# The GLA state-times-query product on operands split in two, in two of three token blocks

## The chip, the cores and the metric

One core of a Trainium2 chip runs the whole program. The metric is the device time of one execution in microseconds (us); the kernel before has a median of 1791.93 us over three runs (1784.84 to 1792.70).

## The reference, cut to what matters

One decoder layer over 2048 prompt tokens and 64 sample tokens, width 1024. A projection `x @ w_in` feeds two branches, a sliding-window attention and a gated linear attention (GLA); both are gated, projected, merged and normalised. The GLA branch is what the change touches. It has 4 heads with 128 key channels and 256 value channels, and walks over chunks of tokens with a state `S` (128 x 256) per head:

```
def step(S, xs):
    qc, kc, vc, gc = xs
    b = jnp.cumsum(gc, axis=1)
    b_last = b[:, -1]
    qt = qc * jnp.exp(b)
    kt = kc * jnp.exp(-b)
    kend = kc * jnp.exp(b_last[:, None] - b)
    o_inter = jnp.einsum('bthk,bhkv->bthv', qt, S)
    A = jnp.where(causal, jnp.einsum('bthk,bshk->bhts', qt, kt), 0.0)
    o_intra = jnp.einsum('bhts,bshv->bthv', A, vc)
    S = jnp.exp(b_last)[..., None] * S + jnp.einsum('bshk,bshv->bhkv', kend, vc)
    return S, o_inter + o_intra
```

The kernel takes chunks of 128 tokens. `o_inter`, the state times the query, is the product that changes.

## The kernel before, in words

**The matrix products.** All tokens (2112) are cut in three token blocks `s` = 0, 1, 2 of 704. The main loop runs over `groups`: each is one weight block times one activation block, 4 (or 2) k-steps of three matmuls each (L1326, L1327, L1328), since every operand is held as a high and a low part in the 32-bit type fp32r and the product is high*high + high*low + low*high. `split` (L142, L143) makes the parts: ScalarE casts the value to fp32r, and VectorE subtracts that from the value. Most products use a seven-product scheme, whose sums of weight blocks GpSimd makes (L348) and whose sums of activation blocks VectorE makes (`cx`, L465). The loop order is the order on TensorE, and it is fixed by hand. On the other engines and on SyncE's DMA queue a list scheduler sets the order at build time.

**The side work.** Attention and GLA ride along: `at(t, f)` files a function under a tick, one tick is four k-steps of the main loop (12 matmuls), and `tick()` runs what is due. GLA work for block `s` is filed by `gla_phase`: for each head and each piece of up to 256 tokens a dictionary `B`, and for each of its chunks `i`, `st` ticks apart, `gla_v` and `gla_a`, then 5/3 `st` later `gla_b`, then 10/3 `st` after the first `gla_c`. Before these come the loads of the piece (`gla_load`, `gla_load_v`: `gin`, `zkq`, `zvv`), `gla_z` (a scan and exponentials of the gates, L1030 to L1047) and, three ticks ahead of the first chunk, `gla_kq`, which multiplies keys and queries with them (L1058, L1060). Its result `qb` lies in the tile named `gb`.

**The product.** `gla_b` opens a PSUM accumulation with `qb` times the state in plain fp32 (L1110), adds the three products of the split scores `ah` and values `gv`, `gl` (L1104, through `three`), makes the state update in a second PSUM tile in the same way, and VectorE then writes the new state (L1118). The outputs of the first chunk of a head in block 0 have no state product.

**Tiles.** `mtile("fin")` is the ring of result tiles: ten tiles of 128 x 352 in which the results of the main loop wait for their way to memory (`fin`, `th`, `part`), and which the gate work also uses (`zg`, `gin`). `wp` are six tiles of split weights, `ws` ten of raw ones, `r` the raw activations from `xT`. The main loop writes four PSUM tiles `pd` in turn, the side work four named `pa`.

Of the kernel before, what the change touches and what calls it, by code (L numbers as in the profile page):

```python
# [13 lines left out]
F32R = mybir.dt.float32r  # L14
# [24 lines left out]
HV = 256  # L39
# [4 lines left out]
MS = NT // (2 * MT)  # L44
# [13 lines left out]
def kernel(ctx, tc, io):  # L58
    nc = tc.nc
    mm = nc.tensor.matmul  # L60
# [15 lines left out]
    def pa():  # L76
        return psa.tile([P, 512], F32, tag="pa", name="pa")

    T = MT

    def mtile(tag, dt=F32, name=None):
        n, bufs = {"xb": (4 * T, 16), "a": (T, 7), "fin": (T, 10), "ws": (512, 10), "wp": (D, 6)}[tag]
        pool = px if tag == "xb" else pr
        return pool.tile([P, n], dt, tag=tag, name=name or tag, bufs=bufs)
# [6 lines left out]
    def mpool(name):  # L91
        mid.close()
        M["name"] = name
        M["p"] = mid.enter_context(tc.tile_pool(name=name, bufs=1, side="left", reuse_waits="tile"))

    def mt(tag, n, bufs, dt=F32, name=None):
        return M["p"].tile([P, n], dt, tag=tag, name=name or tag, bufs=bufs)
# [26 lines left out]
    def at(t, fn):  # L124
        side.setdefault(max(int(t), now[0]), []).append(fn)
# [15 lines left out]
    def split(dst_h, dst_l, src, eng=nc.vector):  # L141
        pin["a"] = nc.scalar.copy(dst_h, src)  # L142
        i = eng.tensor_tensor(dst_l, src, dst_h.bitcast(F32), ALU.subtract)  # L143
        if eng is nc.vector:
            pin["d"] = i
# [111 lines left out]
    for n, (kind, s, kh, prs) in enumerate(sets):  # L257
        start_of.append(len(groups))
        base.append(int(tk))
        for pr_ in prs:  # L260
# [5 lines left out]
            elif seq[n] in PLAIN:  # L266
                jk = [(j, k) for j in range(2) for k in range(2)]
                for c in range(2):
                    for j, k in jk if kind == "a" else [(j, k) for k, j in jk]:
                        q, p = pr_[j]  # L270
# [428 lines left out]

    def gate_load(B):  # L700
        x = B["x"] = mtile("fin", name="gin")
        s, t = B["s"], B["t"]
        g = gl_d.rearrange("(a b r) t -> b a r t", a=2, b=2)[t][:, :16, s * T:(s + 1) * T]
        for h in range(GH):
            nc.sync.dma_start(x[32 * h:32 * h + 32], g)

    def gate(B, h0):
        ps = [pa() for _ in range(2)]
        for j in range(2):
            r = slice(32 * (h0 + j), 32 * (h0 + j) + 32)  # L710
            mm(ps[j][:, :T], wgk[r], B["x"][r], start=True, stop=True, tile_position=(32 * (h0 + j), 0))
        for j in range(2):
            h = h0 + j
            z, m = B["z", h], B["m", h] = mtile("fin", name="zg"), mt("lg", T, 4, name="mg")
            nc.scalar.activation(z, ps[j][:, :T], AF.Abs, bias=bgk[:, h:h + 1])
            nc.scalar.activation(m, ps[j][:, :T], AF.Relu, scale=-1.0, bias=nbgk[:, h:h + 1])
# [263 lines left out]
    S_t = [const.tile([P, HV], F32, name=f"S{i}") for i in range(GH + 1)]  # L980
# [11 lines left out]
    def rot(key):  # L992
        r = R[key][cnt[key] % len(R[key])]
        cnt[key] += 1
        return r

    sstate = {}
# [56 lines left out]
    def gla_kq(B):  # L1054
        T, Tp = B["T"], B["Tp"]
        zk, zq = B["zkq"][:, 0], B["zkq"][:, 1]
        for t in (B["k"], B["k2"]):
            nc.vector.tensor_tensor(t[:, :T], zk[:, :T], t[:, :T], ALU.mult)  # L1058
        for t, n in ((B["q"], T), (B["qb"], Tp)):
            nc.vector.scalar_tensor_tensor(t[:, :n], zq[:, :n], HK ** -0.5, t[:, :n], ALU.mult, ALU.mult)  # L1060

    def gla_v(B, i):
        n = P if i < B["nt"] else NS
        ts = slice(i * P, i * P + n)
        tp = pa()
        for m in range(2):
            nc.tensor.transpose(tp[:n, m * P:(m + 1) * P], B["zvv"][:, m, ts], ident)  # L1067
        nc.tensor.transpose(tp[:n, HV:HV + HK], B["k2"][:, ts], ident)
        if n == P:
            B["gv", i] = rot("gv"), rot("gl")  # L1070
            split(*B["gv", i], tp[:, :HV + HK])
            return
        g = mt("pr2", 2 * GU, 6, name="gs")[:, :HV + HK]
        nc.scalar.copy(g[:n], tp[:n, :HV + HK])
        nc.vector.tensor_copy(g[NS:], tp[:n, :HV + HK])
        B["gv", i] = g[:, :HV], g[:, HV:]

    def gla_a(B, i):
        ts = slice(i * P, (i + 1) * P)
        ap = pa()  # L1080
        mm(ap[:, :P], B["k"][:, ts], B["q"][:, ts], start=True, stop=True)  # L1081
        A_ = rot("a")
        nc.vector.copy_predicated(A_, cmask.bitcast(U32), ap[:, :P])
        x = rot("ah")
        split(x[:, :P], x[:, P:], A_, nc.gpsimd)
        B["a", i] = x[:, :P], x[:, P:]

    def gla_norm(B, key, o, n):
# [6 lines left out]
        nc.scalar.mul(on[:n], o, sq[:n])  # L1095
        B["on", key] = on

    def gla_b(B, i):
        ts = slice(i * P, (i + 1) * P)
        gh, gl = B["gv", i]  # L1100

        def three(ps, w, x, start):
            for j, (a, c) in enumerate(((w[0], x[0]), (w[1], x[0]), (w[0], x[1]))):
                mm(ps, a, c, start=start and j == 0, stop=(j == 2))  # L1104

        gv, kT2 = (gh[:, :HV], gl[:, :HV]), (gh[:, HV:], gl[:, HV:])
        S = sstate.get(B["h"])
        op = pa()
        if S is not None:
            mm(op[:, :HV], B["qb"][:, ts], S_t[S], start=True, stop=False)  # L1110
        sp = pa()
        three(sp[:, :HV], kT2, gv, True)
        three(op[:, :HV], B["a", i], gv, S is None)
        Sn = S_free.popleft()
        if S is None:
            nc.vector.tensor_copy(S_t[Sn], sp[:, :HV])
        else:
            nc.vector.scalar_tensor_tensor(S_t[Sn], S_t[S], B["e1"][:, i:i + 1], sp[:, :HV], ALU.mult, ALU.add)  # L1118
            S_free.append(S)
        sstate[B["h"]] = Sn  # L1120
        gla_norm(B, i, op[:, :HV], P)
# [59 lines left out]
    def gla_phase(s, t0, st):  # L1181
        at(t0, lambda: mpool(f"cg{s}"))
        at(t0, rings)
        nu = sum(-(-T_ // P) for _, T_ in GCH[s]) * GH
        b0 = t0 + 14
        u = 0
        for h, (c0, T_) in ([(h, c) for c in GCH[s] for h in range(GH)] if s == 1 else
                            [(h, c) for h in range(GH) for c in GCH[s]]):
            if True:
                last = c0 + T_ == NT  # L1190
                Tp = T_ - (NS if last else 0)
                nt = Tp // P
                B = dict(h=h, t0=c0, T=T_, Tp=Tp, nt=nt, last=last)
                tt = lambda v: b0 + st * v + 0.01
                b = tt(u)
                at(b - 13, lambda B=B: gla_load(B))
                at(b - 10, lambda B=B: gla_load_v(B))
                at(b - 8, lambda B=B: gla_z(B))
                at(b - 3, lambda B=B: gla_kq(B))
                for i in range(nt):  # L1200
                    at(tt(u + i), lambda B=B, i=i: gla_v(B, i))
                    at(tt(u + i), lambda B=B, i=i: gla_a(B, i))
                    at(tt(u + i + 5 / 3), lambda B=B, i=i: gla_b(B, i))
                    at(tt(u + i + 10 / 3), lambda B=B, i=i: gla_c(B, i, P, i * P))
                at(tt(u + 1) + 3, lambda B=B: gla_load_g(B))
                o = tt(u + nt)
                u += nt
                if last:
                    u += 1
                    at(o - 5, lambda B=B: samp_state(B))  # L1210
                    at(o, lambda B=B: gla_v(B, B["nt"]))
                    at(o + 2, lambda B=B: samp_a(B))
                    at(tt(u - 1 + 0.5) + 2, lambda B=B: nc.sync.dma_start(io["o_sp"][B["h"]], S_t[sstate[B["h"]]]))
                    o = max(o + 6, tt(u - 1 + 4 / 3) + 1)
                    at(o, lambda B=B: samp_b(B, 0))
                    at(o + 2, lambda B=B: samp_b(B, 2))
                    at(o + 5, lambda B=B: gla_c(B, "s", NS, B["Tp"]))
                    at(max(o + 6, tt(u + 4 / 3) + 1), lambda B=B: gla_store(B))
                else:
                    at(tt(u + 7 / 3) + 1, lambda B=B: gla_store(B))  # L1220
        return int(b0 + st * (nu + 7 / 3) + 3)

    for s in range(MS):
        for t in range(2):
            B = dict(s=s, t=t)
# [6 lines left out]
    t0 = 90  # L1232
    tiles = [sum(-(-n // P) for _, n in c) * GH for c in GCH]
    st = (base[U2] - 3 - t0 - 160 - 17 * MS) / sum(n + 7 / 3 for n in tiles)
    for s in range(MS):
        t0 = gla_phase(s, att_phase(s, t0), st)
# [55 lines left out]
    def rest_m(t, u, n, last):  # L1292
        return [part(f, samples=last) for f in load_m(t, u, n, last)]
# [5 lines left out]
    for g, (n, q, i, s, p, b, ch) in enumerate(groups):  # L1299
# [15 lines left out]
        w = wps.pop(g)  # L1315
# [3 lines left out]
        ps = (banks[b] if b < 4 else banks2[b - 4])[:, :T]  # L1319
        if n == U2 and g >= start_of[U2] + 16:  # L1320
            ps = banks2[b][:, :T]
        for k in range(q.kh):
            ks, ts = slice(k * P, (k + 1) * P), slice(k * T, (k + 1) * T)
# [12 lines left out]
        if n == U2:  # L1336
# [7 lines left out]
            if d == 3:  # L1344
                ox = M["p"]
                xf, x, xr0 = load_m(1, 0, TM), [], []
# [101 lines left out]
    for j, (t, u, n) in enumerate(order):  # L1448
# [9 lines left out]
        for r in tiles:  # L1458
            if r is tiles[-1] and j + 1 < len(order):
                x = rest_m(*order[j + 1], last=(j + 2 == len(order)))  # L1460
# [124 lines left out]
```

## Time and profile before

| | before |
|---|---|
| median of three runs | 1791.93 us (1784.84 to 1792.70) |
| the profiled execution | 1783.34 us, its span 1781.6 us |
| busy: PE, DVE, ACT, POOL | 1752.0, 1085.9, 851.7, 374.5 us |
| granted TensorE clock, mean | 0.997 |

The profile is of one execution. PE is TensorE's matmuls and PEld its weight loads; DVE is VectorE, ACT ScalarE, POOL GpSimd, SP the queue from which most DMAs are issued. A row of a group gives line, engine, operation, output and input tile, shapes, count, then busy time and mean duration, then idle time before it and what ended that. Since matmuls overlap, the duration of one is more than the time to the start of the next; the cost on PE is read from starts. `x2` at a plain fp32 matmul stands for two records of one instruction. GLA of block 0 lies between about 350 and 590 us, of block 1 between about 765 and 1035 us, of block 2 after 1200 us. Line numbers are those of the kernel before.

### The profile page before, as it was taken

The page shows a single profiled execution, that of the slowest core. Times are in us where ns is not written, and L with a number is a line of the kernel's source. Part 1 is how long each engine was busy: PE and PEld are TensorE (multiplying, and loading weights), DVE is VectorE, ACT ScalarE, POOL GpSimd, SP SyncE. Part 2 cuts the span into 40 slices and gives each one's busy share as a digit, 9 for nine tenths or more (in the row PEclk, how much of TensorE's full clock was granted, in tenths as well). Part 3 has the DMA queues.
Part 4 walks back from the last instruction along what each step waited for, and adds up shares of the span by engine and source line. Part 5 has one row for each costly group of instructions (what it writes and reads, how often), then busy time and mean ns, then how long its engine had stood idle before and what let it go on. Part 6 is the DMA issues. An engine that isn't in the chain of part 4 may idle for free.

```text
span 1781.6 us, 31643 instructions
## 1 busy us (share of the span) xinstructions
PE 1752.0 (98%) x11026; PEld 1644.8 (92%) x11026; DVE 1085.9 (61%) x2146; ACT 851.7 (48%) x2052; POOL 374.5 (21%) x522
## 2 busy tenths in 40 slices
PE   8999999998999999999999999999999999999998
PEld 8999988997999988999999998899999999998887
DVE  6656678778555466547655336635766755536666
ACT  4575656556574365446567334645533432311100
POOL 5345533454111000004211100000123132111111
PEclk9999999999999999999999999999999999999999
DMA  6789966976978987887789798779989978965531
GB/s 216 272 317 332 330 232 224 319 279 207 311 261 279 304 258 231 269 286 228 255 266 319 239 294 279 237 244 318 298 267 244 301 212 223 332 148 194 171 104 54
DMA packets 290911, 452.33 MB, mean 254 GB/s; under 512 B 29213, under 2 KB 210133, under 8 KB 290736
## 3 DMA queue, kind: packets, MB, share of 16 engines
q1 hardware_dynamic: 262896, 415.04, 70.7%
q10 hardware_dynamic: 20464, 26.24, 4.2%
q0 software_dynamic: 7392, 9.04, 3.6%
q8 instruction: 87, 1.43, 0.3%
q14 instruction: 72, 0.59, 0.1%
HBM read 297.52 MB, written 153.57 MB: 253 GB/s over the span
## 4 chain that ended last, share of the span: by engine, by line
PE 74%; DMA 2%; DVE 1%; POOL 1%; ACT 1%; issue 1%; SPq 0%; DVEq 0%; ACTq 0%; POOLq 0%
PE pd L1326 17%; PE pd L1328 17%; PE pd L1327 16%; PE pd L1389 3%; PE pd L1390 3%; PE pd L1391 3%; PE pa L1104 2%; PE pa L1110 1%; PE pa L777 1%; PE pa L823 1%; PE pa L809 1%; PE pa L1127 1%; DMA r<-ug_d 1%; PE pa L1067 1%; PE pa L1081 1%; PE pa L1326 1%
## 5 line engine op out<-in xcount | busy, mean ns | idle before, releaser
L143 DVE TENSOR_TENSOR wp<-ws,wp 128x512 fp32r<-128x512 f32 (+1 forms) x396 | 274.4, 696 | 203.9 <-ACT wp L142 192.9
L142 ACT CAST wp<-ws 128x512 fp32r<-128x512 f32 (+1 forms) x396 | 234.2, 595 | 191.8 <-PE pd L1328 127.7
L348 POOL TENSOR_TENSOR ws<-ws 128x256 f32<-128x256 f32 x162 | 144.1, 918 | 156.5 <-DVE wp L143 103.9
L143 POOL TENSOR_TENSOR ah<-aper,ah 128x128 fp32r<-128x128 f32 x64 | 37.3, 583 | 397.6 <-ACT ah L142 394.4
L384 ACT COPY m<-pd 128x352 f32<-128x352 f32 x146 | 66.1, 454 | 87.2 <-PE pd L1328 80.0
L1390 PE MATMUL pd<-woh,x 128*128 128x512 f32 (+1 forms) x272 | 102.4, 377 | 0.0
L1391 PE MATMUL pd<-wol,x 128*128 128x512 f32 (+1 forms) x272 | 102.4, 377 | 0.0
L1389 PE MATMUL pd<-woh,x 128*128 128x512 f32 (+1 forms) x272 | 102.4, 377 | 0.0
L1326 PE MATMUL pd<-x1h,wp 128*128 128x352 f32 x292 | 96.7, 331 | 2.3 <-DVE fin L405 2.2
L1326 PE MATMUL pd<-x7h,wp 128*128 128x352 f32 x292 | 97.1, 333 | 1.1 <-DVE fin L201 0.9
L1326 PE MATMUL pd<-x3h,wp 128*128 128x352 f32 x292 | 96.8, 331 | 0.3 <-DVE fin L399 0.3
L1326 PE MATMUL pd<-x5h,wp 128*128 128x352 f32 x292 | 96.6, 331 | 0.0
L1326 PE MATMUL pd<-x6h,wp 128*128 128x352 f32 x292 | 96.3, 330 | 0.0
L1326 PE MATMUL pd<-x2h,wp 128*128 128x352 f32 x292 | 96.3, 330 | 0.0
L1326 PE MATMUL pd<-x4h,wp 128*128 128x352 f32 x292 | 96.2, 330 | 0.0
L1328 PE MATMUL pd<-x1h,wp 128*128 128x352 f32 x292 | 94.0, 322 | 0.1
L1328 PE MATMUL pd<-x7h,wp 128*128 128x352 f32 x292 | 94.0, 322 | 0.0
L1328 PE MATMUL pd<-x4h,wp 128*128 128x352 f32 x292 | 93.8, 321 | 0.0
L1328 PE MATMUL pd<-x3h,wp 128*128 128x352 f32 x292 | 93.8, 321 | 0.0
L1327 PE MATMUL pd<-x7l,wp 128*128 128x352 f32 x292 | 93.8, 321 | 0.0
L1328 PE MATMUL pd<-x6h,wp 128*128 128x352 f32 x292 | 93.8, 321 | 0.0
L1328 PE MATMUL pd<-x5h,wp 128*128 128x352 f32 x292 | 93.8, 321 | 0.0
(454 smaller groups left out, 5387.9 us busy)
## 6 DMA issues: line engine op xcount, KB each, us to landing
wp<-wk_w_g SPq DMA_DIRECT2D x96, 512.0 KB
ws<-w_g SPq DMA_DIRECT2D x120, 256.0 KB
wk_w_g<-wp SPq DMA_DIRECT2D x48, 512.0 KB
wp<-wk_w_ra SPq DMA_DIRECT2D x32, 512.0 KB
wp<-wk_w_rg SPq DMA_DIRECT2D x32, 512.0 KB
ws<-w_at SPq DMA_DIRECT2D x53, 256.0 KB
wp<-wk_w_at SPq DMA_DIRECT2D x24, 512.0 KB
ws<-w_pg SPq DMA_DIRECT2D x48, 256.0 KB
```

The source lines that it names most:

```text
L142: pin["a"] = nc.scalar.copy(dst_h, src)
L143: i = eng.tensor_tensor(dst_l, src, dst_h.bitcast(F32), ALU.subtract)
L348: nc.gpsimd.tensor_tensor(o[:, c], x[:, c], y[:, c], op)
L384: nc.scalar.copy(A[i], ps)
L777: mm(ps[kv][:, j, k0:], A["zq"][r, g0 + j, :], A["kk"][r, 0, k0:], start=True, stop=True, tile_position=(kv * HD, 0))
L1104: mm(ps, a, c, start=start and j == 0, stop=(j == 2))
L1326: mm(ps, wh, xh[:, ts], start=first, stop=False, skip_group_check=ch)
L1327: mm(ps, wh, xl[:, ts], start=False, stop=False, skip_group_check=ch)
L1328: mm(ps, wl, xh[:, ts], start=False, stop=(k == q.kh - 1 and not (type(i) is tuple and i[1] == 0)), skip_group_check=ch)
L1389: mm(ps, xh[:, xs], hi, start=(k == 0), stop=False)
L1390: mm(ps, xl[:, xs], hi, start=False, stop=False)
L1391: mm(ps, xh[:, xs], lo, start=False, stop=(k == KT - 1))
```

## The change

In blocks 0 and 1 the state product is made like the others: query and state are split in high and low parts, and three fp32r matmuls take the place of one fp32 matmul. Block 2 keeps the fp32 product.

```
--- before.py
+++ after.py
@@ gla_kq
             nc.vector.scalar_tensor_tensor(t[:, :n], zq[:, :n], HK ** -0.5, t[:, :n], ALU.mult, ALU.mult)
+        if B["s"] < MS - 1:
+            B["qs"] = [mtile("fin", F32R, n) for n in ("qbh", "qbl")]
+            split(B["qs"][0][:, :T], B["qs"][1][:, :T], B["qb"][:, :T])
@@
+    def gla_s(B):
+        S = sstate.get(B["h"])
+        if S is not None and "qs" in B:
+            B["Ss"] = [mt(n, HV, 1, F32R) for n in ("Sh", "Sl")]
+            split(*B["Ss"], S_t[S])
+
     def gla_b(B, i):
...
-        def three(ps, w, x, start):
+        def three(ps, w, x, start, last=True):
             for j, (a, c) in enumerate(((w[0], x[0]), (w[1], x[0]), (w[0], x[1]))):
-                mm(ps, a, c, start=start and j == 0, stop=(j == 2))
+                mm(ps, a, c, start=start and j == 0, stop=(last and j == 2))
...
-        if S is not None:
+        if S is not None and "qs" in B:
+            three(op[:, :HV], [q[:, ts] for q in B["qs"]], B["Ss"], True, False)
+        elif S is not None:
             mm(op[:, :HV], B["qb"][:, ts], S_t[S], start=True, stop=False)
@@ gla_phase
-                B = dict(h=h, t0=c0, T=T_, Tp=Tp, nt=nt, last=last)
+                B = dict(s=s, h=h, t0=c0, T=T_, Tp=Tp, nt=nt, last=last)
...
                     at(tt(u + i), lambda B=B, i=i: gla_a(B, i))
+                    at(tt(u + i + 1), lambda B=B: gla_s(B))
                     at(tt(u + i + 5 / 3), lambda B=B, i=i: gla_b(B, i))
```

The query's parts `qbh` and `qbl` take two tiles of the ring `fin` per piece, from `gla_kq` to the piece's last `gla_b`. The state's parts `Sh` and `Sl` have one buffer each; they are made anew for each chunk, two thirds of `st` ahead of its `gla_b`. Block 0 has 20 chunks of which 16 have a state, block 1 has 24: 40 products change. There are 24 pieces, 20 of 256 tokens and 4 of 128.

On PE the place of one such product, in block 0, before:

```order
L1328 MATMUL pd_74<-x5h,wp 128x352
L1110 MATMUL pa<-S_219,gb 128x256
L1104 MATMUL pa<-gv 128x256
L1104 MATMUL pa<-gv,gl 128x256
L1104 MATMUL pa<-gl,gv 128x256
L1104 MATMUL pa<-gv,ah 128x256 x2
L1104 MATMUL pa<-gl,ah 128x256
```

and now:

```order
L1340 MATMUL pd_74<-x5h,wp 128x352
L1113 MATMUL pa<-Sh,qbh 128x256
L1113 MATMUL pa<-Sh,qbl 128x256
L1113 MATMUL pa<-Sl,qbh 128x256
L1113 MATMUL pa<-gv 128x256
L1113 MATMUL pa<-gv,gl 128x256
L1113 MATMUL pa<-gl,gv 128x256
L1113 MATMUL pa<-gv,ah 128x256 x2
L1113 MATMUL pa<-gl,ah 128x256
```

One row becomes three, and nothing else on PE moves. On the other engines the list scheduler places the 128 new instructions and shifts others. On SP's queue in block 0, before (`zkq`, `zvv` and `gin` are loads of later GLA pieces, `ws` raw weights, `r` raw activations, `wk_w_rg` stores of split weights, `sg` a load of the gate of the output):

```order
L314 DMA ws<-w_at 128x512
L1012 DMA zkq<-z_kq_89 128x2x256
L314 DMA ws<-w_at 128x512
L442 DMA r_4676<-xT 128x4x352
L371 DMA wk_w_rg_4602<-wp 128x1024
L371 DMA wk_w_rg_4641<-wp 128x1024
L1009 DMA gin<-zg_d 128x256
L314 DMA ws<-w_at 128x512 x2
L1018 DMA zvv<-z_vv_93 128x2x256
```

and now:

```order
L314 DMA ws<-w_at 128x512
L1012 DMA zkq<-z_kq_89 128x2x256
L1018 DMA zvv<-z_vv_93 128x2x256
L1009 DMA gin<-zg_d 128x256
L314 DMA ws<-w_at 128x512
L442 DMA r_4698<-xT 128x4x352
L371 DMA wk_w_rg_4620<-wp 128x1024
L371 DMA wk_w_rg_4663<-wp 128x1024
L314 DMA ws<-w_at 128x512 x2
```

The loads `zvv` and `gin` now stand ahead of the load of `r`. On DVE a little later, ahead of the write of the state that ends the stretch, before:

```order
L1047 COPY e_4932<-gb 128x2
L1058 TENSOR_TENSOR em<-zkq,em 128x256
L143 TENSOR_TENSOR wp<-ws,wp 128x512
L1058 TENSOR_TENSOR ek<-zkq,ek 128x256
L1060 SCALAR_TENSOR_TENSOR dm<-zkq,dm 128x256
L143 TENSOR_TENSOR x4l<-cx,x4h 128x704
L1060 SCALAR_TENSOR_TENSOR gb<-zkq,gb 128x256
L143 TENSOR_TENSOR x4l<-cx,x4h 128x704
L1118 SCALAR_TENSOR_TENSOR S_223<-S_222,e_4472,pa 128x256
```

and now:

```order
L1047 COPY e_4970<-gb 128x2
L465 TENSOR_TENSOR cx<-r_4917,cx 128x704
L1140 TENSOR_TENSOR sg<-pa,sg 128x2x128
L143 TENSOR_TENSOR wp<-w_4972,wp 128x512
L143 TENSOR_TENSOR wp<-ws,wp 128x512
L465 TENSOR_TENSOR cx<-r_4917,cx 128x704
L143 TENSOR_TENSOR x4l<-cx,x4h 128x704
L143 TENSOR_TENSOR wp<-ws,wp 128x512
L143 TENSOR_TENSOR x4l<-cx,x4h 128x704
L1129 SCALAR_TENSOR_TENSOR S_223<-S_222,e_4484,pa 128x256
L143 TENSOR_TENSOR wp<-ws,wp 128x512
L1058 TENSOR_TENSOR em<-zkq,em 128x256
```

The seven steps of `gla_z` and `gla_kq` that one piece had in this stretch on DVE (L1030, L1035, L1036, L1058 twice, L1060 twice) now stand before or behind it: the scan, `dm` and both steps on `ek` ahead of the step on `cx` that waits for `r`, the other three behind the write of the state. The split of this chunk's state (`Sl`) stands four rows ahead of the piece shown.

## The prediction

> **What bounds the kernel now.** First the page's busy times, then the stretches in which the change acts.
>
> ```profile
> span 1781.6 us, 31643 instructions
> PE 1752.0 (98%) x11026; PEld 1644.8 (92%) x11026; DVE 1085.9 (61%) x2146; ACT 851.7 (48%) x2052; POOL 374.5 (21%) x522
> ```
>
> TensorE is busy nearly all of the time; DVE and ACT have room on average. An average hides stages, so the second view is the busy time by stretch (columns: stretch, length, then PE, PEld, DVE, ACT, POOL with their counts, granted clock, DMA share, GB/s).
>
> ```profile
> core 0: us, PE busy (x) PEld busy (x) DVE busy (x) ACT busy (x) POOL busy (x), PEclk, DMA share, GB/s
> 340.00:396.00 56.00, 55.04 (x356) 54.15 (x355) 40.60 (x74) 34.28 (x81) 24.48 (x35) 1.00 0.86 303
> 396.00:430.00 34.00, 27.62 (x179) 23.38 (x178) 30.43 (x56) 21.80 (x52) 18.55 (x22) 0.95 0.58 183
> 430.00:600.00 170.00, 170.00 (x1102) 165.98 (x1101) 88.16 (x197) 95.84 (x229) 25.98 (x47) 1.00 0.85 278
> 740.00:1040.00 300.00, 300.00 (x1959) 293.25 (x1959) 169.71 (x354) 167.06 (x398) 51.93 (x88) 1.00 0.82 271
> ```
>
> Two regimes. From 430 to 600 and from 740 to 1040 PE is never idle: time saved on PE comes off the end, and DVE and ACT are 52 to 57% busy. From 396 to 430 PE is idle for 6.4 of 34 us while DVE is 90% busy: there the other engines set the pace. PE's waits over both say who is late:
>
> ```profile
> PE pd L1326 <- DVE fin L405: 2.2, 2, 1.6
> PE pa L544 <- DVE S L1118: 2.2, 1, 2.2
> PE pa L1104 <- DVE aper L1083: 2.0, 1, 2.0
> ```
>
> All of them are DVE, and these make the 6.4 us between them. The chain of waits shows what DVE itself hung on (start, length, what):
>
> ```profile
> 384.81 7.27 DMA r<-xT
> 392.10 0.91 DVE cx L465
> 393.03 0.78 ACT x7h L142
> ...
> 395.99 1.44 POOL w L348
> ...
> 412.62 0.61 DVE gb L1030
> 413.26 0.42 DVE dm L1035
> ...
> 421.40 0.48 DVE S L1118
> 421.92 3.74 PE pa L544 x32
> ```
>
> A load of raw activations lands at 392.1, then GpSimd's sums of weights run until 410, and then DVE works a row of steps off, those of a GLA piece among them, until the state's write frees a PSUM tile for PE.
>
> **The product on PE.** One of the 60 state products and what follows it, in order of time:
>
> ```profile
> 505.93 0.33 PE L1328 MATMUL pd<-x5h,wp 128*128 128x352 f32 x1
> 506.09 0.59 PE L1110 MATMUL pa<-S,gb 128*128 128x256 f32 x2
> 506.33 0.47 PE L1104 MATMUL pa<-gv 128*128 128x256 f32 x1
> 506.64 0.28 PE L1104 MATMUL pa<-gv,gl 128*128 128x256 f32 x1
> 506.76 0.28 PE L1104 MATMUL pa<-gl,gv 128*128 128x256 f32 x1
> 506.88 0.40 PE L1104 MATMUL pa<-gv,ah 128*128 128x256 f32 x2
> 507.12 0.28 PE L1104 MATMUL pa<-gl,ah 128*128 128x256 f32 x1
> ```
>
> Read from starts, an fp32r matmul of this shape costs 0.12 us (506.64 to 506.76, five times over to 507.24). From the start of the fp32 product to the second L1104 it is 0.55 us; less one fp32r matmul, the fp32 product costs 0.43. Three fp32r matmuls cost 0.36. Each changed product thus gives PE 0.07 us. Of the 40, four come before 430 us (376 to 412), where PE waits for DVE soon after; I count those as nothing. The other 36 lie in the full stretches: 36 x 0.07 = 2.5 us less. The bounds: 0, if each is lost in a wait behind it, and 40 x 0.07 = 2.8.
>
> The Trainium skill (FP8 and Floating Point Precision, TensorE Precision Notes) has true FP32 as four passes through the array, high and low crossed. By that rule alone three passes would cost three quarters of 0.43, or 0.32, and the 36 would give 3.9 us. The trace agrees that the product is dear, but a single fp32r matmul takes 0.12 here and not a quarter of 0.43; the rows decide, and the sum keeps 2.5.
>
> **The splits.** 40 of the state and 24 of the query, each a cast on ACT and a subtraction on DVE. The nearest rows are the splits of half a weight tile, of the same shape:
>
> ```profile
> L143 DVE TENSOR_TENSOR wp<-ws,wp 128x256 fp32r<-128x256 f32 x48 | 19.8, 418 | 14.9 <-ACT wp L142 14.9
> L142 ACT CAST wp<-ws 128x256 fp32r<-128x256 f32 x48 | 19.1, 404 | 37.8 <-PE pd L1328 37.7
> ```
>
> Taking 0.42 and 0.40 us for all 64 (four are half as wide), that is at most 26.9 us on DVE and 25.6 on ACT, over 480 to 500 us in which each has over 200 us free. In the full stretches I cost them at nothing. What hides them is the distance to their use. A state is written on DVE and next used in the following chunk:
>
> ```profile
> 508.80 0.46 DVE L1118 SCALAR_TENSOR_TENSOR S<-S,e,pa 128x256 f32<-128x256 f32 x1
> 516.54 0.70 PE L1110 MATMUL pa<-S,gb 128*128 128x256 f32 x2
> ```
>
> Between 509.26 and 516.54 lie 7.3 us for 0.82 us of split; if the queues of ACT and DVE ran over 6.4 us late, PE would wait for `Sl` with everything behind it.
>
> **The stretch 376 to 430.** Two edits of the scheduler pull against each other here. On SP's queue `zvv` and `gin` now go ahead of the load of `r`:
>
> ```profile
> 381.67 0.75 SPq L1012 DMA_DIRECT2D zkq<-z_kq  x1
> 384.38 0.33 SPq L314 DMA_DIRECT2D ws<-w_at  x1
> 384.81 0.39 SPq L442 DMA_DIRECT2D r<-xT  x1
> 389.94 0.42 SPq L1009 DMA_DIRECT2D gin<-zg_d  x1
> 393.01 0.54 SPq L1018 DMA_DIRECT2D zvv<-z_vv  x1
> 387.99 0.41 DVE L1060 SCALAR_TENSOR_TENSOR dm<-zkq,dm 128x256 f32<-128x256 f32 x1
> ```
>
> Their issue takes 0.96 us and their 384 KB, at the 303 GB/s of this stretch, 1.3 us. Ahead of them `zkq` now takes the tile that this step on `dm` reads, so it waits for it. If the step stayed where it was, `r` would be issued at 388.4 + 0.75 + 0.96 + 0.33 = 390.4, 5.6 us late; but DVE has it earlier now, ahead of the splits of `x1` that began at 382.8, and I take no lateness from that: 2.3 us later at the head of the chain, between 0 and 7. DVE also gets two splits of a state and one of a query ahead of the state's write, 1.3 us. Against that the piece's seven steps leave the stretch from 411.8 to 421.4: as they stand in the trace some 0.4 each and the scan 0.6, close to 3 us, of which the three that now follow it may be missed later. Sum: +2.3 + 1.3 - 3 = +0.6. Of the signs I am not sure; the bounds are -3 (the steps leave, nothing is late) and +8 (7 and 1.3).
>
> A rule that speaks against the change belongs here. In these rows GpSimd and DVE run side by side, and DVE's steps are slow:
>
> ```profile
> 397.38 1.43 POOL L348 TENSOR_TENSOR ws<-ws 128x256 f32<-128x256 f32 x2
> 398.11 1.24 DVE L143 TENSOR_TENSOR wp<-ws,wp 128x512 fp32r<-128x512 f32 x1
> ```
>
> and over all of the line's groups (min/median/max ns):
>
> ```profile
> L143 DVE TENSOR_TENSOR wp<-ws,wp x396: 408/691/1296, 25.5 to 1568.8; 128x512 fp32r<-128x512 f32 x174, 128x256 fp32r<-128x256 f32 x24
> ```
>
> A subtraction with a median of 0.69 us takes 1.24 there. The Trainium skill (SBUF — State Buffer, SBUF: two separate sides) says why it may: a VectorE operation with two SBUF inputs and a GpSimd operation that reads SBUF exclude each other for a whole instruction. The added subtractions are of that kind. At 1.24/0.69 the three would cost 2.3 instead of 1.3, and the total would be 1 us more; the sum leaves them at 1.3.
>
> **The ring of result tiles.** The query's parts hold two of ten tiles. Chunks are 10.45 us apart (506.09 to 516.54), a tick is 12 matmuls of 0.16 (505.93 to 506.09), or 1.9. A piece of two chunks holds its parts for 3 ticks and 1 + 5/3 chunks, 34 us, out of 21: 3.2 tiles on average, up to four or six at once. A store from the ring takes 4.8 us:
>
> ```profile
> DMA to landing us min/median/max: 3.4/4.8/7.3
> ```
>
> ```profile
> 480.00:530.00 50.00, 6.21 (x13) 2.88 (x6) 0.00 (x0) 1.00 0.83 280
> ```
>
> This row is the view by stretch for the tile `fin` alone: 13 writes on DVE and 6 on ACT in 50 us, each holding a tile for some 6 us, make 2.3 tiles, and the gates add up to four. That is 6 to 9 or 10 of ten. A wait for a tile would hold ACT or DVE, and behind it the copies that free PSUM. PE has four PSUM tiles, so three products of 1.9 us, 5.8 us, go by before it notices. I cost the ring at nothing, with that as the cover.
>
> **The sum.** -2.5 + 0.6 = -1.9 us: 1783.3 becomes 1781.4 in the profiled execution's terms. That execution lay 8.6 us below the median of the three runs, which is what will be compared: 1791.9 - 1.9 = 1790.0.
>
> **The rivals.**
> *The ring runs full (slower).* Around 505 to 550 and 925 to 970 a result finds no free tile until a query's parts are given up at the piece's last product. A wait of one chunk, 10.45 us, costs PE 10.45 - 5.8 = 4.7. For: the count above comes to ten. Against: the store that frees the next tile lands in 4.8 us, under the cover. It decides from three such waits: 14 us, 1804.
> *The split state is late (slower).* One buffer for `Sh` and `Sl`, the cast behind other work in ACT's queue. If PE waited 0.3 us at each of 40, 12 us would eat the gain: about 1802. Against: the 6.4 us of slack. This is the case in which the change doesn't do what it says.
> *`r` is late (no change).* SP waits for `zkq`'s tile, all 7 us arrive at the chain's end: 1790.0 + 4.7 = 1795.
> *The idle time of 396 to 430 goes too (faster).* The DVE steps that leave were what PE waited for. All 6.4 us and 2.8: 9.2 less, 1782.7.
>
> **How the numbers follow.** 0.5%, 9 us, is about what a measurement of this kernel tells from no change; the three runs alone span 7.9. My forecast, a change too small to see, has 0.67; `r` late 0.13, also within; the ring 0.09 and the late state 0.04 slower; the idle time gone 0.07. So faster 0.07, same 0.80, slower 0.13. The range: below, the lowest run shown less 2.5 and the 3 of the lower bound, 1779.3; above, the median less 2.5 plus 8 is 1797.4, and the nearer half of the ring's case takes it to 1801.
>
> **What would show it.** Right: three L1113 starts 0.12 apart in place of the fp32 product, PE full from 430 to 600 and 740 to 1040, no PE wait for ACT or DVE named `Sl` or `Sh`. The load of `r` landing at 393 to 395, and PE idle 4 to 8 us from 396 to 430. Wrong: PE waits above 3 us in the full stretches behind a `fin`, `th` or `zg`; or a granted clock that differs.

## The result: slower by 0.74%

| | before | after |
|---|---|---|
| time, median | 1792.18 us (1784.84 to 1792.70) | 1803.28 us (1797.51 to 1808.17) |
| ratio after/before, 95% interval | | 1.0074 (1.0050 to 1.0097) |
| profiled execution: time, span | 1783.3, 1781.6 us | 1803.79, 1801.9 us |

Against some 1790 us the ratio is 13 us, between 9 and 17. The prediction had 1790.0 us, with 1801.0 as its upper end: it was wrong. Among the runs below, one execution of e8 (4557.6 us) and one of e17 (2150.33 us, at a granted clock of 0.75) were slow and are left out of medians and ratios. The profile after, first its page:

```profile
span 1801.9 us, 31833 instructions
PE 1756.9 (98%) x11066; PEld 1647.9 (91%) x11066; DVE 1112.1 (62%) x2210; ACT 866.7 (48%) x2114; POOL 379.0 (21%) x522
```

PE works 4.9 us longer, at a mean granted clock of 0.995 instead of 0.997, and is idle for 45.0 us instead of 29.6. Where it is idle, the view by stretch says (stretch, length, then PE, PEld, DVE, ACT, POOL with counts, granted clock, DMA share, GB/s):

```profile
396.00:430.00 34.00, 26.99 (x186) 23.74 (x185) 30.01 (x51) 20.11 (x47) 21.53 (x24) 1.00 0.64 205
430.00:600.00 170.00, 165.62 (x1078) 160.65 (x1079) 98.56 (x224) 99.19 (x253) 26.80 (x48) 1.00 0.82 270
740.00:1040.00 300.00, 293.93 (x1922) 284.35 (x1921) 181.09 (x381) 171.70 (x421) 52.88 (x84) 0.99 0.80 263
```

The stretch that the prediction worried about, 396 to 430, has about as much idle PE as before, 7.0 us against 6.4. The two that were full, 430 to 600 and 740 to 1040, now have 4.4 and 6.1 us of idle PE. PE's waits between 340 and 1070 us name the late engine (waiting instruction, what came late: us in all, times, longest):

```profile
PE pa L1138 <- DVE S L1129: 5.2, 4, 2.2
PE pa L1113 <- DVE sg L1140: 3.3, 2, 2.1
PE pa L1113 <- DVE Sl L143: 1.5, 2, 1.1
PE pa L1113 <- ACT Sh L142: 1.0, 1, 1.0
```

Only the last two lines are waits for the state's parts, 2.5 us, and both lie ahead of 430. The large ones are waits for a PSUM tile that DVE's write of the state (L1129) or of the gated output (L1140) gives back. DVE is busy for 58 and 60% of the two stretches, so on average it is not short of time. It waits itself; the same view for DVE's scan L1030, the first step of a GLA piece, before:

```profile
DVE gb L1030 <- DMA gin<-zg_d: 5.4, 3, 4.4
DVE gb L1030 <- PE pa L1110: 4.0, 3, 1.9
```

and after:

```profile
DVE gb L1030 <- DMA gin<-zg_d: 31.6, 11, 7.4
```

Before, the scan waited three times for its output tile `gb`, until PE's last L1110 had read it. After, that wait is gone, and the scan waits for the load `gin` eleven times where it did so three times. One of these waits in the chain of waits of after (start, length, what):

```profile
882.11 0.38 SPq L321
882.49 0.05 issue
882.54 7.22 DMA gin<-zg_d
889.76 0.02 issue
889.78 0.70 DVE gb L1030
890.51 0.42 DVE dm L1035
890.93 0.34 DVE ek L1036
891.27 0.40 DVE S L1129
891.72 0.44 PE pa L1138 x2
```

SP issues the load behind weight loads (L321), 7.2 us later it lands, the scan and two more steps of the next piece run, and only then the state write, for whose PSUM tile PE has waited 2.2 us. The same piece before, in order of time:

```profile
870.75 0.38 SPq L1009 DMA_DIRECT2D gin<-zg_d  x1
...
881.18 0.69 DVE L1030 TENSOR_TENSOR_SCAN gb<-rmask,gin 128x256 f32<-128x256 f32 x1 [1.80 <-PE pa L1110]
881.79 0.46 DVE L1118 SCALAR_TENSOR_TENSOR S<-S,e,pa 128x256 f32<-128x256 f32 x1
```

The load was issued 10.4 us ahead of the scan. After, DVE stood at the scan from 882.4, ahead of its load: the scan has come forward by one state write in DVE's order (28 writes ahead of it, 29 before). The same count for others: in block 0, state writes ahead of the fourth to twelfth scan were 1, 4, 5, 6, 8, 9, 11, 13, 14 before and are 0, 2, 5, 5, 7, 8, 11, 13, 14 now.

Theory **early release**: in the kernel before, `gb` is the query of the state product, and PE holds its tile until the piece's last chunk. With the split, nothing reads `gb` after `qbl`, the tile comes free at once, and the scheduler brings the next scan forward in DVE's queue, where it blocks the state writes while its load is on the way. Its rival, **ring**: the parts hold fin tiles, and results and gates wait for stores.

A caution on single profiles: the first 60 us, before and after, where the change has done nothing yet:

```profile
0.00:60.00 60.00, 53.49 (x316) 49.68 (x317) 41.61 (x54) 31.62 (x57) 23.90 (x39) 1.00 0.62 211
```

```profile
0.00:60.00 60.00, 49.89 (x286) 45.18 (x287) 40.55 (x53) 29.89 (x53) 22.95 (x37) 0.94 0.60 200
```

In that time PE starts 286 products instead of 316, with 3.6 us more idle time and a granted clock of 0.94: at 0.16 us each, an estimate, the execution is 4 to 5 us late from the start. This comes with the execution, not with the change: two kernels below that are the kernel before but for unused bytes (e11, e12) have 0.94 too, and one with the whole change (e18) has 1.00. Times are therefore compared by medians over the runs, and profiles from 340 us on only.

### The profile page after: what moved, and what is told of

The parts are those of the page before. It is cut to its first block, busy times and chain, and to the rows that moved or that the text cites. A ratio compares the mean times of both kernels' runs of the same rounds, so it can differ in the third digit from the quotient of the medians.

```text
span 1801.9 us, 31833 instructions
## 1 busy us (share of the span) xinstructions
PE 1756.9 (98%) x11066; PEld 1647.9 (91%) x11066; DVE 1112.1 (62%) x2210; ACT 866.7 (48%) x2114; POOL 379.0 (21%) x522
## 4 chain that ended last, share of the span: by engine, by line
PE 46%; DVE 2%; ACT 2%; DMA 2%; issue 1%; POOL 1%; SPq 0%; DVEq 0%; ACTq 0%; POOLq 0%
PE pd L1338 9%; PE pd L1340 9%; PE pd L1339 9%; PE pd L1401 3%; PE pd L1402 3%; PE pd L1403 3%; PE pa L1113 2%; PE pa L1340 1%; PE pa L1338 1%; PE pa L1339 1%; PE pa L777 1%; PE pa L823 1%; DMA r<-ug_d 1%; PE pa L1138 1%; PE pa L1121 0%
## 5 line engine op out<-in xcount | busy, mean ns | idle before, releaser
L1338 PE MATMUL pd<-x5h,wp 128*128 128x352 f32 x292 | 96.6, 331 | 0.0
L1338 PE MATMUL pd<-x4h,wp 128*128 128x352 f32 x292 | 96.2, 330 | 0.0
L1339 PE MATMUL pd<-x6l,wp 128*128 128x352 f32 x292 | 94.3, 323 | 0.0
L1339 PE MATMUL pd<-x3l,wp 128*128 128x352 f32 x292 | 94.0, 322 | 0.0
```

Source lines behind the costliest of these rows:

```text
L1338: mm(ps, wh, xh[:, ts], start=first, stop=False, skip_group_check=ch)
L1339: mm(ps, wh, xl[:, ts], start=False, stop=False, skip_group_check=ch)
```

## The experiments

### Hold the tile, hold the ring, release early, move the scan

**e1**, `gb` held by a GpSimd read behind the piece's last norm:

```
+        if "qs" in B and i == B["nt"] - 1:
+            nc.gpsimd.tensor_tensor(small([P, 1], "held"), B["sq"], B["qb"][:, :1], ALU.add)
```

> The changed kernel, with the query's tile gb kept until its piece's last gla_norm by a one-column GpSimd read, as long as before; splits, product and the two fin tiles stay. In the order on DVE the scans of L1030 then stand behind as many state writes as before, or one more (in the second token block 2, 4, 5, 7, 8, 10, 12, 13, 15 writes so far ahead of scans four to twelve; before 1, 4, 5, 6, 8, 9, 11, 13, 14; in the changed kernel 0, 2, 5, 5, 7, 8, 11, 13, 14). Theory 'early release' (the tile that comes free early lets DVE take up the next scan ahead of its load, and the states wait behind it): the scan's wait for gin falls from 50 us in all to under 15 us, PE's idle time between 340 and 1070 us falls by about 10 us, the time is 1789 to 1795 us. Theory 'ring' (two to four of the ten fin tiles are gone and results and gates wait for stores): no change, 1801 to 1805 us.

(The counts quoted there are those of block 0, the first. The 50 us of waits named there are 31.6 by the view above, or 35.3 over the whole execution.)

**e2**, the kernel before with two fin tiles held per piece:

```
+            B["rt"] = [mtile("fin", name=n) for n in ("rt0", "rt1")]
+            for t in B["rt"]:
+                nc.scalar.copy(t[:, :1], B["qb"][:, :1])
...
+            for t in B["rt"]:
+                nc.gpsimd.tensor_tensor(small([P, 1], "held"), B["sq"], t[:, :1], ALU.add)
```

> The kernel before, with two fin tiles taken at gla_kq of each piece of the first two blocks and held until its last gla_norm (one column written by ACT, read by GpSimd): no split, no new product, the order on DVE as before. It leaves nothing of the result out. Theory 'early release': 1791 to 1795 us, since only results and gates wait a little for stores (some 17 us of ACT's and DVE's own waiting, most of it hidden). Theory 'ring': 1799 to 1805 us, the whole loss.

**e3**, the kernel before with `gb` given up early:

```
+            q = mt("qc", GU, 2, name="qc")
+            nc.scalar.copy(q[:, :T], B["qb"][:, :T])
+            B["qb"] = q
```

> The kernel before, with the query copied once (ACT, fp32) into a tile of its own at gla_kq, PE reads the copy: gb comes free as early as in the changed kernel, the scans stand in DVE's order as early as there (0, 2, 5, 5, 7, 8, 11, 12, 14 state writes ahead of scans four to twelve), but no part is split, no fin tile is used and the product stays plain fp32. Theory 'early release': scans wait some 40 to 50 us for gin, and the time is 1799 to 1806 us. Theory 'ring': as before, 1790 to 1794 us.

**e4**, the scan kept from moving forward. `pin["d"]` is the last subtraction that `split` put on DVE ahead of it, of a weight or of another operand:

```
+        with tc.issue_after(pin["d"].ins):
             nc.vector.tensor_tensor_scan(b[:, :Tp], ...)
```

> The changed kernel, with each scan of L1030 issued only behind the last weight split written ahead of it, so that the scheduler can't bring it forward; gb still comes free early and the fin tiles are used. In the order on DVE 1, 4, 6, 7, 9, 11, 12, 14, 16 state writes stand ahead of scans four to twelve. Theory 'early release', of which the place of the scan in the queue is the acting part: waits for gin under 10 us, the time 1788 to 1796 us; where the scan comes so late that its own gates are late for PE, up to 1800 us with PE waiting for kb or qb instead. Theory 'ring': 1801 to 1805 us.

| | time, us | ratio to before (95%) |
|---|---|---|
| e1 | 1809.32 | 1.0106 (1.0074 to 1.0138) |
| e2 | 1807.09 | 1.0099 (1.0068 to 1.0130) |
| e3 | 1804.16 | 1.0086 (1.0052 to 1.0120) |
| e4 | 1803.49 | 1.0075 (1.0053 to 1.0098) |

e3 came out as early release says: no split, no ring, and the whole loss. Its scans wait even longer than the 40 to 50 us foretold:

```profile
DVE gb L1030 <- DMA gin<-zg_d: 56.7, 15, 10.0
```

e4 missed early release's range and lies in that of its rival; more on it at e8. e1 and e2 missed both theories, and their profiles say why. In e1 the scan's waits for `gin` are 3.9 us, in e2 5.6, both as before. But in both, every product on PE was slower, down to the last block, which neither touches. From 1100 to 1250 us PE is never idle, so the count of its products in 150 us shows its speed; in the runs below whose `x` and `r` were not moved it is 1062 to 1070, since the same products do not fall into the window in each. Before, then e1, then e2:

```profile
1100.00:1250.00 150.00, 150.00 (x1069) 140.17 (x1068) 83.56 (x185) 81.31 (x214) 2.35 (x5) 1.00 0.83 270
```

```profile
1100.00:1250.00 150.00, 150.00 (x1050) 138.13 (x1051) 82.87 (x179) 76.72 (x209) 0.92 (x2) 1.00 0.83 270
```

```profile
1100.00:1250.00 150.00, 150.00 (x1054) 137.91 (x1053) 84.78 (x183) 77.46 (x210) 0.92 (x2) 1.00 0.82 266
```

The granted clock is 1.00 in all three. What the two share is the little tile `held`, three times 32 bytes in the pool of constants, which lies below the activations `x` and `r` in SBUF: it moved them up by 96 bytes.

### Where the operands lie

**e5**, the kernel before with 96 unused bytes in that place (written once, never read):

```
+        if "pad" not in pin:
+            pin["pad"] = small([P, 24], "pad", 1)
+            nc.gpsimd.memset(pin["pad"][:], 0.0)
```

> The kernel before, with one unused tile of 96 bytes per partition in the pool of constants, so that every tile behind it in SBUF (the x and r tiles, moving operands of all large products, among them) lies 96 bytes higher, as in the two experiments with the GpSimd read, where it was the side effect of that read's own little tile; the weights' pool stays where it was. Nothing is computed otherwise, no instruction moves. Theory 'address' (the place of the moving operand sets how fast the products follow each other): starts of successive 352-column products lie 162.2 ns apart instead of 159.4 (as in both experiments), PE's busy time rises by 18 to 22 us, the time is 1806 to 1812 us. Theory 'run' (that spacing came from the GpSimd reads or from a slower stretch of the chip): 159.4 ns and 1785 to 1795 us.

1804.22 us, ratio 1.0085 (1.0068 to 1.0103). That is less than theory address's 1806 to 1812, but far from its rival's 1785 to 1795, and nothing but addresses and one small memset was changed:

```profile
1100.00:1250.00 150.00, 150.00 (x1049) 138.57 (x1048) 82.81 (x180) 79.33 (x216) 0.92 (x2) 1.00 0.83 267
```

So e1 and e2 had measured two things at once. Three more placed the effect, the kernel before each time; e10 and e12 have the same memset. **e10**: `small([P, 16], "pad", 1)`, 64 bytes.

> The kernel before with an unused tile of 64 bytes per partition in the pool of constants: x and r tiles stay at 32 modulo 64. Theory 'moving operand at 0 modulo 64 is slow': product spacing 159.4 ns, the time as before, 1786 to 1794 us. Theory 'any shift': 162.2 ns and 1802 to 1808 us.

**e11**: 32 bytes at the end of the right-hand pool, which moves weights and fin tiles down by 32.

```
+    pr.tile([P, 8], F32, tag="pad", name="pad", bufs=1)
```

> The kernel before with an unused tile of 32 bytes at the end of the right-hand pool: weights (wp, ws), m, u and fin tiles move from 32 to 0 modulo 64, x and r stay at 32. Theory 'moving operand': 159.4 ns, 1786 to 1794 us. Theory 'x and weights must lie alike modulo 64': 162.2 ns, 1802 to 1808 us.

**e12**: e5 and e11 together.

> Both pads: x, r and GLA's tiles 96 bytes higher (0 modulo 64), weights and fin at 0 modulo 64 too. Theory 'moving operand': 162.2 ns, 1802 to 1808 us. Theory 'x and weights must lie alike': 159.4 ns, 1786 to 1794 us.

| | x, r modulo 64 | weights modulo 64 | mean distance of starts, ns | time, us | ratio (95%) |
|---|---|---|---|---|---|
| before | 32 | 32 | 159.4 | 1789 to 1790 | |
| e5 | 0 | 32 | 162.3 | 1804.22 | 1.0085 (1.0068 to 1.0103) |
| e10 | 32 | 32 | 159.9 | 1791.10 | 1.0010 (0.9993 to 1.0027) |
| e11 | 32 | 0 | 160.5 | 1794.89 | 1.0023 (1.0007 to 1.0040) |
| e12 | 0 | 0 | 159.6 | 1791.56 | 1.0013 (0.9997 to 1.0030) |

(Distance of starts of successive 352-column products, over those 150 to 172 ns apart, some 650 in each stretch of 150 us. From stretch to stretch of one execution it varies, from 159.3 to 159.7 in the kernel before and from 159.1 to 160.5 in e12.) With moving operand and weights alike modulo 64 the products run at about the speed of the kernel before, at 0 as at 32. Apart they do not, and the loss is larger when it is the activations that moved; e11's 160.5 and its time lie between the two theories it was to tell apart. Why is open. The rows of e11 and e12 in the same stretch:

```profile
1100.00:1250.00 150.00, 150.00 (x1064) 140.15 (x1063) 83.72 (x188) 81.35 (x216) 1.50 (x3) 1.00 0.83 266
```

```profile
1100.00:1250.00 150.00, 150.00 (x1068) 140.15 (x1067) 83.78 (x185) 81.71 (x216) 2.35 (x5) 1.00 0.84 275
```

The changed kernel itself is untouched by this: its `x`, `r` and weights lie where they lay before.

### The first round again, without the shift

In **e6** and **e7**, e1 and e2 are built with the read's tile in the GLA stage's own pool (`mt("held", 1, 3)` for `small([P, 1], "held")`). **e8** is e4 with the scan pinned in the first two blocks alone (`if B["s"] < MS - 1`).

> As the first experiment (the changed kernel with gb kept until the piece's last gla_norm), but the one-column tile of the GpSimd read lies in the GLA stage's own pool, so that no address of an x or r tile differs from the changed kernel's. Theory 'early release': product spacing 159.4 ns, gin waits of the scan under 6 us, PE's idle time 32 to 36 us in all, the time 1786 to 1793 us. Theory 'ring', or splits as such: 1800 to 1806 us.

> As the second experiment (the kernel before, with two fin tiles held from gla_kq to the piece's last gla_norm), the GpSimd read's tile in the GLA stage's own pool, the addresses of x and r as before. Theory 'early release': 1789 to 1794 us. Theory 'ring': 1799 to 1806 us.

> As the fourth experiment (the changed kernel, scans of L1030 not brought forward), but in the first two token blocks only: in the fourth experiment PE fell back by some 10 us between 1290 and 1440 us, in the third block, which the change doesn't touch, and about 6 us between 340 and 1070 us. Theory 'early release': 1791 to 1797 us, with the third block as before. Theory 'ring': 1800 to 1805 us.

e7: 1793.40 us, ratio 1.0016 (1.0000 to 1.0031). The ring alone is a small term, 3 us (0 to 6), and its profile has it in one place (a result waits for a store, behind it a gate, behind that PE):

```profile
519.12 0.52 DVE L201 SCALAR_TENSOR_TENSOR fin<-th,pd 128x352 f32<-128x352 f32 x1 [3.03 <-DMA z_ga<-fin]
519.73 0.55 ACT L715 ACTIVATE zg<-pa,bgk 128x352 f32<-128x352 f32 x1 [3.72 <-DVE fin L201]
520.78 1.31 PE L711 MATMUL pa<-gin,wgk 32*128 32x352 f32 x4 [1.64 <-ACT mg L716]
```

e6: 1797.35 us, 1.0052 (1.0036 to 1.0069). That lies between the ranges of the two theories: less was gained than early release had foretold, and since the interval overlaps that of the changed kernel, it is not even clear that any was. Its own read is part of that: the waits for `gin` are down to before's, but the scan now waits for GpSimd, whose queue comes to the read late.

```profile
DVE gb L1030 <- POOL held L1134: 13.1, 10, 3.3
DVE gb L1030 <- DMA gin<-zg_d: 4.7, 2, 2.4
```

e8: 1800.09 us, 1.0052 (1.0032 to 1.0072), missing early release's 1791 to 1797 as e4 missed its range. Both times lie where the rival had put them, though e7 shows that the ring is too small for that. The scan waits for no load in e4 and e8, and yet in e8 PE is idle for 12.2 us between 340 and 1070, against 7.3 before: 3.0 of it behind weights, 2.1 behind a write of the state where before has 2.2, 1.9 behind gates, 0.8 behind `Sh`, and the rest in small waits. What takes over when the scan is put later by force was not settled.

**e9**, the changed kernel with the parts in the unit ring, where `gin` and `gb` lie (`unit(F32R, n)` for `mtile("fin", F32R, n)`):

> The changed kernel, with the query's parts qbh and qbl in the ring of GLA's unit tiles (u, ten tiles, where gin, gb and the gates lie) instead of the ring of result tiles: splits, products and the early end of gb stay, but the ring of fin is as before, and the unit tiles that the parts hold keep the next piece's gb as late as in the kernel that holds gb (in the order on DVE 2, 4, 5, 7, 8, 10, 12, 13, 15 state writes ahead of scans four to twelve). Theory 'early release' with the ring as a small second term: both costs gone, PE's step at 517 to 530 us of before (3.3 us with gb held, 2.7 us with two fin tiles held) goes away, PE idle 30 to 34 us, the time 1788 to 1793 us. If splits and late states cost by themselves: 1796 to 1799 us, as with gb held alone.

1799.42 us, 1.0057 (1.0038 to 1.0076): a miss for early release. The parts crowd that ring instead: SP's issue of `gin` (L1009) now waits for PE's L1113, which reads the parts, and the scan waits again:

```profile
SPq L1009 <- PE pa L1113: 8.1, 6, 3.8
DVE gb L1030 <- DMA gin<-zg_d: 14.9, 6, 4.0
```

### What is left: the splits or the product

**e13** has all the splits but the old product, which keeps `gb` by reading it:

```
-        if S is not None and "qs" in B:
-            three(op[:, :HV], [q[:, ts] for q in B["qs"]], B["Ss"], True, False)
-        elif S is not None:
+        if S is not None:
             mm(op[:, :HV], B["qb"][:, ts], S_t[S], start=True, stop=False)
```

**e14** drops the query's split from e13 (`B["qs"] = 1` in place of its tiles and split). **e15** is e6, **e16** is e9, each with `nc.gpsimd` as the engine of the new subtractions.

> The changed kernel with all its splits, but the state's product is the plain fp32 one of the kernel before, from gb and S themselves: nothing reads qbh, qbl, Sh and Sl, gb is held by the product until the piece's last chunk, the scans stand in DVE's order as before. If the rest of 0.5% is the work of the splits on ACT and DVE (and the fin tiles): 1795 to 1800 us. If it is the new product and its wait for the state's parts: 1789 to 1794 us.

> The kernel before with the splits of the state alone (one cast on ACT, one subtraction on DVE for each product with the state; nothing reads them), no split of the query, no fin tiles. If the splits' work counts in proportion to their number: 1793 to 1797 us. If not, or if only the query's split in its fin tiles counts: 1789 to 1793 us.

> The changed kernel with gb held (as in the sixth experiment) and the subtractions of state and query on GpSimd instead of DVE. If DVE's extra work is the rest: 1788 to 1794 us. If the state's low part, which GpSimd makes more slowly, is late for the product: 1797 to 1804 us with PE waiting for Sl.

> The changed kernel with the query's parts in the unit ring (as in the ninth experiment) and the subtractions of state and query on GpSimd. If DVE's extra work is the rest: 1786 to 1792 us, the best of the versions with the new product. If the state's low part is late for the product: 1797 to 1804 us with PE waiting for Sl.

| | time, us | ratio to before (95%) |
|---|---|---|
| e13 | 1792.78 | 1.0024 (1.0007 to 1.0040) |
| e14 | 1789.65 | 1.0007 (0.9992 to 1.0022) |
| e15 | 1796.86 | 1.0050 (1.0032 to 1.0067) |
| e16 | 1803.76 | 1.0088 (1.0058 to 1.0117) |

All splits together with their fin tiles cost 4 us (1 to 7), and e13 lies below the 1795 to 1800 us foretold for the case that they are the whole rest; those of the state alone cost nothing that shows. Moving the subtractions off DVE does not give the rest back: e15 is no faster than e6, and e16 is slower than e9 (scan's waits for `gin` 24.8 us). Nor is it the other reading, a late `Sl`: PE's waits for it are 0.3 us in e15 and 0.5 in e16. But the work then lies on GpSimd (in e15 busy for 181.0 us between 340 and 1070, 132.8 in e6), so neither run shows what it costs on DVE.

### The tile held where PE held it

Both with a read on DVE, right behind the state write of the piece's last chunk, which needs no other engine. **e17** is e3 with it, **e18** the changed kernel with it:

```
+        if "qs" in B and i == B["nt"] - 1:
+            add(mt("held", 1, 3), S_t[Sn][:, :1], B["gb"][:, :1], ALU.add)
```

> The third experiment (the kernel before with the query copied to a tile of its own, which PE reads), but gb is kept until a one-column read on DVE right behind the state write of its piece's last chunk. The copies stay. If the early end of gb made the loss of the third experiment (1804 us): 1789 to 1794 us, PE's waits between 340 and 1075 us 5 to 8 us instead of 15.2. If the copies or their tile did: 1800 to 1806 us.

> The changed kernel (splits, new product, fin tiles) with gb kept by the same read on DVE instead of GpSimd's behind the norm. If GpSimd's read gave gb up too late in the sixth experiment (1797 us): 1789 to 1793 us, by the sum of the splits' 4 us and the product's -3 us. If not: 1795 to 1799 us again.

| | time, us | ratio to before (95%) |
|---|---|---|
| e3, released early | 1804.16 | 1.0086 (1.0052 to 1.0120) |
| e17, the same, held | 1788.21 | 0.9997 (0.9980 to 1.0015) |
| changed kernel | 1803.28 | 1.0074 (1.0050 to 1.0097) |
| e18, the same, held | 1791.95 | 1.0017 (1.0000 to 1.0035) |

Both as early release foretold, e17 even just below its range, with 4.0 us of PE's waits where 5 to 8 were expected. Twenty-four copies and a tile of their own cost nothing that shows; when `gb` comes free makes all of e3's loss and some three quarters of the change's, 10 of 13 us. The scan's waits in e17 and e18:

```profile
DVE gb L1030 <- DMA gin<-zg_d: 6.0, 3, 4.3
```

```profile
DVE gb L1030 <- DMA gin<-zg_d: 4.9, 2, 2.7
```

PE's busy time over both blocks of the change, in before, after, e3, e17 and e18, one row each:

```profile
340.00:1070.00 730.00, 722.66 (x4680) 692.09 (x4678) 428.28 (x871) 407.04 (x993) 120.94 (x190) 1.00 0.82 269
```

```profile
340.00:1070.00 730.00, 711.85 (x4636) 681.02 (x4635) 451.45 (x926) 416.63 (x1046) 130.53 (x194) 1.00 0.80 263
```

```profile
340.00:1070.00 730.00, 714.58 (x4609) 683.00 (x4608) 426.32 (x863) 410.70 (x1009) 124.46 (x194) 1.00 0.81 264
```

```profile
340.00:1070.00 730.00, 725.92 (x4704) 696.93 (x4703) 437.70 (x901) 416.17 (x1019) 125.88 (x193) 1.00 0.82 270
```

```profile
340.00:1070.00 730.00, 719.88 (x4703) 690.47 (x4702) 456.09 (x960) 422.43 (x1056) 126.81 (x191) 1.00 0.82 268
```

Of 730 us PE is idle for 7.3, 18.2, 15.4, 4.1 and 10.1: the two that release early stand out; of the two that hold, e17 is below before and e18, with splits and ring, between. The same by position: how many us later than before the same main product starts, found by matching the products in order.

| | at 342 us | 430 | 530 | 860 | 950 | 1070 |
|---|---|---|---|---|---|---|
| after | 4.9 | 3.8 | 9.6 | 9.0 | 18.3 | 17.7 |
| e3 | 5.1 | 2.5 | 9.1 | 11.1 | 15.0 | 15.7 |
| e17 | 3.3 | -0.6 | -0.6 | -0.6 | -0.6 | -0.6 |
| e18 | 0.8 | 0.0 | 2.7 | 1.9 | 2.9 | 2.3 |
| e7 | 1.7 | -1.5 | 2.6 | 2.6 | 2.6 | 2.6 |

What e18 still loses up to 530 is where e7 loses it: the ring's one place, with the same wait of PE's for the gate.

```profile
PE pa L711 <- ACT mg L716: 2.0, 1, 2.0
```

What these pairs show is that the loss hangs on when `gb` comes free. That it goes by the scan's waits for its load is argued: the waits come and go with the loss (56.7 against 6.0 us, 31.6 against 4.9), and the chain at 882 us shows one of them reach PE. But e4 and e8 have no such waits and lose all the same, so this path is not shown to be the only one.

No version with the new product beats the kernel before; e18, the best, is 2.7 us above it, and its interval touches 1.

## Why the prediction was wrong

The terms, in its own order:

- **The product on PE, -2.5: right.** From the start of a product to that of the main loop's next matmul, with six fp32r matmuls between, a median of 1148 ns became 1073 where `gb` is held (e6; in after 1072.5): 75 ns each, 3.0 us for 40. Three starts lie 0.11 to 0.12 apart as foretold:

```profile
500.75 0.28 PE L1113 MATMUL pa<-Sh,qbh 128*128 128x256 f32 x1
500.87 0.27 PE L1113 MATMUL pa<-Sh,qbl 128*128 128x256 f32 x1
500.98 0.28 PE L1113 MATMUL pa<-Sl,qbh 128*128 128x256 f32 x1
501.10 0.28 PE L1113 MATMUL pa<-gv 128*128 128x256 f32 x1
```

  By the Trainium skill's four passes (FP8 and Floating Point Precision, TensorE Precision Notes) the 40 would have given 4.3 us, an estimate. Measured were 3.0.
- **The splits, nothing: small.** With the ring 4 us (e13, 1 to 7), those of the state alone 1 us with zero inside the interval (e14). The cover of 7.3 us held in the full stretches: between 430 and 1070 PE waits for no `Sh` or `Sl`. Ahead of 430 it waits 2.5 us for them, which the prediction had not expected.
- **The stretch 376 to 430, +0.6: inside its bounds.** By position -1.1, within -3 to +8, but one execution does not tell it from nothing: by the table above e7 and e17 gain 3.2 and 3.9 us on the profile before between 342 and 430. PE is idle for 7.0 us, foretold 4 to 8. `r` landed at 398.5; less the 4.9 us by which this execution was already late, 393.6, foretold 393 to 395. (Of the waits said to make up the 6.4 us before, 0.7 lies ahead of 396; a fourth of 0.6, L1127 behind the state's write, completes them.)
- **The ring, nothing: mis-sized by 3 us** (e7, 0 to 6). The cover of 5.8 us was reckoned for a wait that holds up PSUM. The one that counted holds up a gate, which PE takes directly. The 4.8 us for a store came from a row that counts only the 48 stores on GpSimd's queue (L229), all after 1300 us; the store of e7's wait, on SP's queue, takes 4.3 us in its chain, so that figure was near by luck.
- **The sum had no term for what releases `gb`.** That is the step that failed. The prediction listed what the change adds and which rows move between 376 and 430, saw there that "the piece's seven steps leave the stretch", and booked that as 3 us gained. It did not ask why they could leave: because the tile they needed had lost its last reader. The same cause acted on the other pieces, in the stretches called full, where it put the scan ahead of state writes and of its own load. Both were to be seen: the order on DVE, and the wait of the scan for PE L1110, 4.0 us in three waits, which was the brake that the change took off. That brake was worth some 16 us in the kernel before (e3 against e17) and some 10 in the changed kernel (1.0074 against e18's 1.0017). By which waits it reaches PE is shown for single places only, and e4 and e8 leave open what else takes part.

From their own runs the terms are early release +15 (9 to 22, e3), splits with ring +4 (1 to 7, e13) and product -3, together +16, where +13 (9 to 17) was measured; with the 10 us that holding the tile gives back in the changed kernel itself they make +11.

Two rivals came within 2 us of the result by other mechanisms, which is luck: "the ring runs full" gave 1804, and the ring alone costs 3; "the split state is late" gave 1802, and its waits are 2.5 us, in the stretch where they cost little. The sign to look for, PE waits above 3 us behind a `fin`, `th` or `zg`, did not appear: between 340 and 1070 us after has 0.9 us behind `fin` and none behind the others. The list of what would show the forecast wrong lacked a wait on DVE's side.

## What to carry to other kernels

When a change takes away a tile's last slow reader, ask what that reader was holding back: a tile that comes free sooner lets a scheduler pull work forward, and in a queue worked in order an instruction that waits for a load stops what stands behind it (here DVE for 7.4 us, and then PE for 2.2). Where that shows, a one-column read on the engine that owns the order, right behind the step that used to end the hold, puts the brake back at no cost that shows (e17). And look at the addresses after any edit of a pool: 96 bytes in the wrong pool cost about as much here as the change.

## What the hardware showed that was not expected

With moving operand and weights at different places modulo 64 bytes, the fp32r products followed each other every 162.3 ns (activations moved) or 160.5 (weights moved) instead of 159.4, at a granted clock of 1.00. It took 1.8% or 0.7% off PE's rate in these products and added 15 or 4 us to this kernel (e5, e11). Only 0 and 32 were tried. The page shows it only as busy time: PE is 98% busy before and 99% in e5, with 1776.3 us in it instead of 1752.0.
